# A decoder step's input projection started on two feature tiles, its RMS root multiplied in afterwards

## The chip, the cores and the metric

The kernel runs on one core of one Trainium2 chip. The metric is device time in microseconds (us) of one execution, the median of several. Everything is float32 in memory. A float32 product on TensorE is made of three passes: an operand is split into a high half (rounded to the `fp32r` format) and a low half (what the rounding left), and weights-high times data-high, weights-high times data-low and weights-low times data-high are added up in PSUM. The code calls these three matmuls a triple.

## The reference

One inference step of a one-layer decoder for 288 tokens: 256 of a prompt and 8 samples of 4 tokens. D is 2048. Cut to what the change touches:

```python
mod = silu(c) @ w_ada + b_ada             # 9 conditioning rows (prompt, 8 samples) -> 6 x 2048
sh_m, sc_m, gt_m, sh_f, sc_f, gt_f = mod  # shift, scale, gate for the mixer and for the FFN
h    = x * rsqrt(mean(x*x, -1) + 1e-6) * g_mix * (1 + sc_m) + sh_m
proj = h @ w_in                           # 288 x 2048 @ 2048 x 9216
...                                       # gated convolution, spatial gating, w_pa, w_pb, w_out
x    = x + gt_m * (merged @ w_out)
...                                       # second norm, SwiGLU FFN, residual, final norm
```

The mean of squares runs over the 2048 features of a token, so the root is one number for each token, and it needs all of `x`. Shift and scale are one number for each feature and conditioning row: one row for all prompt tokens, and one for each sample.

## The kernel before

Data lie transposed: 128 features on the partitions, 288 tokens along the free axis, so D is 16 *feature tiles*; `w_in` has 72 *output tiles* of 128 columns. A triple is one feature tile times one output tile (288 columns). Its product stands in one of four PSUM banks (`pm`) until a *sink* copies or adds it out; an output tile's partial sum is held in SBUF (`part[m]`, tiles named `s`).

The program is a list of steps. A `Blk` is a block of weights of 1 MB or less: one DMA on SP's queue into one of 7 buffers (`raw`), a *split* in pieces of four tiles (a cast `hi` on ScalarE, ACT, line 400, and a subtraction `lo` on VectorE, DVE, line 402), and its triples on TensorE, PE (lines 215 to 217). An `Ada` block is a piece of `w_ada`: its 4 to 16 float32 matmuls (line 336) add up in one PSUM bank, and the `tail` of the unit's last block copies it out (line 351), adds up its quarters by small matmuls (line 358) and writes `mod` (line 362). A `Do` is any other work, on PE between two triples; `later(f, gap)` holds it until `gap` triples are done. `warm(n)` puts n filler matmuls on data that nobody reads (line 461). A load is issued 7 steps ahead of its step, and a block is split one block ahead. PE's order is the program's. On ACT, DVE, POOL (GpSimd) and SP a scheduler sets it.

The input projection adds up over feature tiles as conditioning arrives, in passes named by their stream (first feature tile, feature tiles in a block, output tiles in a block):

```python
STREAMS = {
    "wA": (0, 1, 8),   # 48 output tiles, feature tile 0
    "wB": (1, 2, 8),   # the same 48, tiles 1 and 2
    "wX": (0, 3, 4),   # the other 24, tiles 0 to 2
    "wC": (3, 5, 3),   # all 72, tiles 3 to 7
    "wD": (8, 8, 2),   # all 72, tiles 8 to 15
```

Between blocks stand the conditioning units: aB in wA (tiles 1, 2), aC and aD in wB and wX (3 to 7), aE in wC (8 to 15).

**The head** is what comes before wA: `x` in four loads (2.36 MB), the two blocks of aA (shift and scale of tile 0 alone), then wA's first block. ACT squares `x` as it lands (line 469), DVE adds the squares up (line 474), PE sums them over the partitions by one-column float32 matmuls (line 481; a float32 matmul stands in the trace as two instructions, in the order below as one), DVE and POOL make the root (line 195), PE broadcasts it over the partitions (line 204), and ACT copies it to SBUF as `rb`, 128 x 288. Then `modulate` makes a tile of `h1`: x times `rb` on DVE (line 248), scale and shift on ACT for the prompt (line 259) and on DVE for the samples (lines 262, 263), the cast on ACT (line 265) and the low half on DVE (line 272). The sinks of wA are plain copies, half of them on ACT (line 521) and half on DVE (line 523); those of wB add (line 526).

Of the kernel before, what the change touches and what calls it, by code (L numbers as in the profile page):

```python
# [83 lines left out]
def _body(tc, nc, d, pc, pw, pslot, ptmp, pps):  # L84
# [166 lines left out]
    def modulate(ks, get, gm, sh0, out):  # L251
        hs, his = {}, {}

        def affine(k, t):
            h = tmp()
            hi = slot(F32R)
            if k == 0 and out is h1:
                A.activation(hi[:, :TP], t[:, :TP], AF.Identity, bias=mod[:, sh0 + k, 0:1], scale=gm[:, k, 0:1])
# [5 lines left out]
            if k == 0 and out is h1:  # L264
                A.copy(hi[:, TP:], h[:, TP:])
            else:
                A.copy(hi, h)
# [37 lines left out]
    class Ada(Step):  # L305
# [68 lines left out]
    class Blk(Step):  # L374
# [11 lines left out]
        cut = None  # L386
# [76 lines left out]
    def squares1():  # L463
        got = S["r1"] = {"ps": psmisc()}
        qs = []
        for a, b in zip(XCUT, XCUT[1:]):
            q = pw.tile([P, 2048], F32, tag="raw", name=nm("q"), bufs=RAW)
            q = q[:, : (b - a) * T].rearrange("p (k t) -> p k t", t=T)
            A.activation(q, x[:, a:b, :], AF.Square)
            qs.append(q)  # L470
        q = S["early"] = qs[0]
        S["late"] = qs[3]
        V.tensor_tensor(q, q, qs[1], ALU.add)
        V.tensor_tensor(q[:, 0:4], q[:, 0:4], qs[2], ALU.add)
        V.tensor_tensor(q[:, 0:2], q[:, 0:2], q[:, 2:4], ALU.add)

    def sums1(late):
        got = S["r1"]
        for q in [S["late"][:, i] for i in range(2)] if late else [S["early"][:, i] for i in (0, 1, 4)]:
            for tb, o in enumerate(TB):  # L480
# [4 lines left out]
                    start=not got.get("on"),  # L485
# [466 lines left out]
```

## Time and profile before

| what | value |
|---|---|
| device time, median of three runs | 1658.42 us (1657.89, 1658.42, 1658.43) |
| the profiled execution: device time | 1658.83 us |
| the profiled execution: span from its first to its last instruction | 1657.1 us |
| mean clock granted to PE, share of full speed | 0.991 |
| busy in the span: PE, DVE, ACT, POOL | 1633.0, 992.7, 745.1, 20.0 us |
| moved by DMA | 357.61 MB, mean 216 GB/s |
| chain that ended last, by engine | issue 52%, PE 46%, DMA 1%, DVE 1%, ACT 1% |

"Issue" in the chain is time in which the engine waited for nothing that the profile shows: here PE going from one matmul to the next. The page's row of 40 slices shows PE at 9 tenths or more from the second slice to the one before the last, with its clock at full; the first slice (41 us) and the last have 7, and the clock is lower there. Times in a timeline are counted from the span's start.

### The profile page before, as it was taken

Reading aid. Unit: us, or ns where it says so; the run is one execution under the profiler, and the core shown is the slowest. Engines: PE = TensorE matmul, PEld = TensorE weight load, DVE = VectorE, ACT = ScalarE, POOL = GpSimd, SP = SyncE. Lnnn points to the kernel's source line nnn. Section 1 sums busy time; section 2 is a strip of 40 time slices with the busy share of each in tenths; the row PEclk is TensorE's granted clock in tenths of the full one; section 3 lists DMA queues with packets and bytes.
Section 4 is the critical chain, followed back from the end, with each engine's and each line's share of the span. In section 5 each row is a group of like instructions: output and inputs, shape, how many; then the busy total and the mean of one; then the engine's idle time right before and its main releaser. Section 6 shows DMA issues by size and latency. Waiting matters only on the chain.

```text
span 1657.1 us, 31287 instructions
## 1 busy us (share of the span) xinstructions
PE 1633.0 (99%) x12559; PEld 1563.6 (94%) x12559; DVE 992.7 (60%) x2070; ACT 745.1 (45%) x1369; POOL 20.0 (1%) x62
## 2 busy tenths in 40 slices
PE   7999999999999999999999999999999999999997
PEld 6899999999899998999999999999999999999997
DVE  3775556877765566667944455555555555555565
ACT  4554335643444434446734444444444444344453
POOL 0000000000000000002000000000000000000000
PEclk7999999999999999999999999999999999999998
DMA  7876766666687667754487546543464434644341
GB/s 295 336 288 241 291 249 250 265 255 254 257 336 278 241 229 273 292 197 154 154 323 270 199 168 211 177 156 128 158 221 162 170 125 154 219 164 169 113 152 58
DMA packets 57122, 357.61 MB, mean 216 GB/s; under 512 B 6384, under 2 KB 9360, under 8 KB 24208
## 3 DMA queue, kind: packets, MB, share of 16 engines
q1 hardware_dynamic: 56688, 355.38, 58.5%
q8 instruction: 98, 1.61, 0.4%
q14 instruction: 48, 0.39, 0.1%
q10 hardware_dynamic: 288, 0.22, 0.0%
HBM read 352.49 MB, written 3.09 MB: 215 GB/s over the span
## 4 chain that ended last, share of the span: by engine, by line
issue 52%; PE 46%; DMA 1%; DVE 1%; ACT 1%; POOLq 0%; POOL 0%; ACTq 0%; DVEq 0%; SPq 0%
PE pm L215 14%; PE pm L216 13%; PE pm L217 13%; PE ada L336 4%; DMA raw<-in_wA 1%; DMA cp<-in_cpack 0%; DVE x L740 0%; PE px L358 0%; PE px L481 0%; PE px L204 0%; DVE lo L402 0%; ACT hi L400 0%; PE px L627 0%; PE px L629 0%; PE px L587 0%
## 5 line engine op out<-in xcount | busy, mean ns | idle before, releaser
L215 PE MATMUL pm<-s,hi 128*128 128x288 f32 (+1 forms) x3760 | 1112.2, 296 | 2.8 <-ACT s L521 1.5
L216 PE MATMUL pm<-s,hi 128*128 128x288 f32 (+1 forms) x3760 | 1107.7, 295 | 0.1
L217 PE MATMUL pm<-s,lo 128*128 128x288 f32 (+1 forms) x3760 | 1106.6, 294 | 0.0
L400 ACT CAST hi<-raw 128x512 fp32r<-128x512 f32 (+1 forms) x966 | 588.9, 610 | 814.6 <-PE pm L216 770.0
L402 DVE TENSOR_TENSOR lo<-raw,hi 128x512 fp32r<-128x512 f32 (+1 forms) x966 | 655.7, 680 | 478.2 <-ACT hi L400 459.0
L215 PEld LDWEIGHTS pm<-s,hi 128*128 128x128 f32 x3760 | 706.9, 188 | 21.1 <-issue 14.8
L217 PEld LDWEIGHTS pm<-s,lo 128*128 128x128 f32 x3760 | 706.7, 188 | 0.0
L216 PEld LDWEIGHTS pm<-s,hi 128*128 128x128 f32 x3760 | 706.1, 188 | 0.3 <-DVE s L272 0.3
L336 PE MATMUL ada<-raw,cs 128*32 128x512 f32 (+2 forms) x960 | 89.4, 517 | 0.0
L526 DVE TENSOR_TENSOR s<-pm,s 128x288 f32<-128x288 f32 x120 | 54.1, 454 | 40.5 <-PE pm L217 40.4
L336 PEld LDWEIGHTS ada<-raw,cs 128*32 128x32 f32 x960 | 28.7, 112 | 43.7 <-issue 38.5
L534 DVE TENSOR_TENSOR s<-pm,s 128x288 f32<-128x288 f32 x72 | 32.9, 456 | 15.0 <-PE pm L217 14.6
L241 ACT CAST s<-t 128x288 fp32r<-128x288 f32 (+1 forms) x76 | 32.6, 433 | 13.9 <-DVE t L566 6.7
L243 DVE TENSOR_TENSOR s<-t,s 128x288 fp32r<-128x288 f32 (+1 forms) x76 | 34.6, 459 | 6.8 <-ACT s L241 6.8
L288 DVE SCALAR_TENSOR_TENSOR x<-pm,mod,x 128x256 f32<-128x256 f32 x80 | 38.0, 475 | 0.0
L712 DVE SCALAR_TENSOR_TENSOR t<-t,pm 128x288 f32<-128x288 f32 x42 | 19.1, 454 | 16.6 <-PE pm L217 16.6
L287 DVE TENSOR_TENSOR t<-pm,mod 128x32 f32<-128x32 f32 x80 | 15.3, 192 | 21.3 <-PE pm L217 21.3
L154 ACT ACTIVATE t<-x 128x288 f32<-128x288 f32 x30 | 13.4, 446 | 20.8 <-DVE x L289 20.8
L159 DVE TENSOR_TENSOR acc<-acc,t 128x288 f32<-128x288 f32 x34 | 15.5, 456 | 8.2 <-ACT t L154 8.2
L521 ACT COPY s<-pm 128x288 f32<-128x288 f32 x45 | 17.0, 399 | 6.7 <-PE pm L217 6.7
L523 DVE COPY s<-pm 128x288 f32<-128x288 f32 x27 | 12.3, 456 | 11.5 <-PE pm L217 11.5
L259 ACT ACTIVATE t<-s,mod,gm 128x256 f32<-128x256 f32 x32 | 18.2, 596 | 2.1 <-DVE s L248 2.1
(110 smaller groups left out, 414.7 us busy)
## 6 DMA issues: line engine op xcount, KB each, us to landing
raw<-in_fi SPq DMA_DIRECT2D x84, 1024.0 KB, 4.9
raw<-in_a SPq DMA_DIRECT2D x64, 1024.0 KB, 9.8
raw<-in_f SPq DMA_DIRECT2D x64, 704.0 KB, 4.1
raw<-in_wD SPq DMA_DIRECT2D x36, 1024.0 KB, 4.9
raw<-in_wC SPq DMA_DIRECT2D x24, 960.0 KB, 4.8
raw<-in_aE SPq DMA_DIRECT2D x16, 1024.0 KB, 8.7
raw<-in_wo SPq DMA_DIRECT2D x16, 1024.0 KB, 5.1
raw<-in_aC SPq DMA_DIRECT2D x8, 1024.0 KB, 9.7
```

The costliest lines, as they stand in the source:

```text
L215: PE.matmul(out, wh, ah, start=first, stop=False)
L216: PE.matmul(out, wh, al, start=False, stop=False)
L217: lh = PE.matmul(out, wl, ah, start=False, stop=last)
L241: A.copy(hi, a)
L243: V.tensor_tensor(lo, a, hi.bitcast(F32), ALU.subtract)
L288: V.scalar_tensor_tensor(x[:, m, :TP], ps[:, :TP], mod[:, gt0 + m, 0:1], x[:, m, :TP], ALU.mult, ALU.add)
L336: PE.matmul(acc[32 * j : 32 * j + 32, :w], cs[:, kt, :], self.raw[:, o : o + w], start=(kt < ks), stop=(kt >= 16 - ks), tile_position=(0, ...
L400: A.copy(hi, self.raw[:, s * 128 : e * 128])
L402: V.tensor_tensor(lo, self.raw[:, s * 128 : e * 128], hi.bitcast(F32), ALU.subtract)
L526: V.tensor_tensor(part[m], ps[:, :T], part[m], ALU.add)
L534: V.tensor_tensor(a, ps[:, :T], a, ALU.add)
L712: V.scalar_tensor_tensor(t, t, 0.5, ps[:, :T], ALU.mult, ALU.mult)
```

## The change

1. *First unit of two tiles, ahead of x.* aA now makes shift and scale of tiles 0 and 1, in four blocks, and is loaded before `x`. aC has tiles 2 to 4, aD 5 to 7. `x` comes in five loads (tiles 0 and 1 first), and wA's first loads stand between them, cut in two or four. Fillers stand between the aA blocks.
2. *32 output tiles without the root.* wA takes feature tiles 0 and 1 for all 72 output tiles, in 9 blocks. In its first four blocks (32 output tiles) the data are `xe`: x times gain and scale, but not times the root (`mk_xe`). `xe` is 298 columns wide: behind the 288 tokens stand the 9 shifts (`mod`) and a zero. When the root is there, `rescale` on POOL multiplies each of these 32 results by `rb` (line 601) and adds the samples' shift column (line 602), in the program 8 tiles after each of wA's 5th to 8th block; `sinkC` adds the prompt's shift column.
3. *The root inside wA.* Squares and their adding are dealt out over the first three blocks (`pace`). PE's sums stand ten triples into wA[2], and the broadcast six triples after them, at wA[2]'s end. `norm1` then makes h1 of tiles 0 and 1, which wA[4] to wA[8] use.
4. *Passes over 2, 3 and 6 tiles.* Output tiles 48 to 71 go by wA, wB (tiles 2 to 4) and wX (5 to 7), tiles 0 to 47 by wA and wC (2 to 7). aC stands after wA's 6th and 8th block, aD after wB's 2nd and 4th. h1 of tiles 2 to 4 is made after wA's 8th block, of 5 to 7 after wB's 4th.
5. *Head in program order.* On ACT, DVE and SP the order is the program's until wA[3].
6. The first wD block runs over the first four feature tiles of both its output tiles, then over the other four (`run_outer`).

```diff
 ADA_UNITS = [
-    ("aA", (16, 16, 0, 0), 1, 8),
-    ("aB", (17, 17, 1, 1), 2, 4),
-    ("aC", (19, 21, 3, 5), 2, 2),
-    ("aD", (23, 23, 7, 7), 1, 8),
+    ("aA", (16, 16, 0, 0), 2, 4),
+    ("aC", (18, 18, 2, 2), 3, 2),
+    ("aD", (21, 21, 5, 5), 3, 2),
...
-EARLY = 48
-XCUT = (0, 5, 10, 14, 16)
+ROOTLESS = 32
+LATER = 48
+XCUT = (0, 2, 6, 10, 14, 16)
 STREAMS = {
-    "wA": (0, 1, 8),
-    "wB": (1, 2, 8),
-    "wX": (0, 3, 4),
-    "wC": (3, 5, 3),
+    "wA": (0, 2, 8),
+    "wB": (2, 3, 4),
+    "wX": (5, 3, 4),
+    "wC": (2, 6, 2),
...
     def squares1():
...
+        return {
+            (0, 5): square(q0, 0),
+            (1, 1): square(q1, 1),
+            (1, 3): add(q1[:, 0:2], q0),
+            (1, 4): square(q2, 2),
+            (1, 6): add(q1, q2),
+            (2, 1): square(q2, 3),
+            (2, 3): lambda: (square(q4, 4)(), add(q1, q2)()),
+        }
...
     def norm1():
         ps = rstd_bcast(S["r1"])
         S["rb1"] = ptmp.tile([P, T], F32, tag="rb", name=nm("rb"), bufs=1)
         A.copy(S["rb1"], ps)
-        xn[0] = normed(0, S["rb1"])
+        mk_h1(0, 2, False).run()
...
+    def mk_xe():
...
+        aA[3].tail(0, lambda: gm_of(0, 2), lambda: weights(1))
+        for f in (scaled, ends):
+            f(0)
+        rest(0)
+        scaled(1)
+        ends(1)
+        rest(1)
+        weights(1)
...
+    def rescale(m0, m1):
+        def f():
+            for m in range(m0, m1):
+                t = raws[m]
+                G.tensor_tensor(t[:, :T], t[:, :T], S["rb1"], ALU.mult)
+                G.tensor_tensor(sam(t[:, TP:T]), sam(t[:, TP:T]), bc4(t[:, T + 1 : T + NC]), ALU.add)
+
+        return Do(f, None)
+
+    def sinkC(m, ps):
+        if m not in raws:
+            return sinkB(m, ps)
+        t = raws.pop(m)
+        V.scalar_tensor_tensor(t[:, :TP], ps[:, :TP], t[:, T : T + 1], t[:, :TP], ALU.add, ALU.add)
+        V.tensor_tensor(t[:, TP:T], ps[:, TP:T], t[:, TP:T], ALU.add)
...
+    steps = [Do(lambda: warm(36)), aA[0], Do(lambda: warm(10)), aA[1], Do(lambda: warm(14)), aA[2], Do(lambda: warm(16)), aA[3]]
+    steps += [Do(mk_xe), Do(lambda: warm(10))]
+
+    def root():
+        later(sums1, 10)
+        later(norm1, 6)
+
+    plan = {2: [Do(root, None)], 6: aC[:4], 8: aC[4:] + [mk_h1(2, 5)]}
+    for i in range(4):
+        plan[5 + i] = [rescale(8 * i, 8 * i + 8)] + plan.get(5 + i, [])
+    steps += at(wA, plan)
+    steps += at(wB, {2: aD[:4], 4: aD[4:] + [mk_h1(5, 8)]})
+    steps += at(wX + wC, {3: aE[:4], 8: aE[4:8], 13: aE[8:12], 18: aE[12:] + [mk_h1(8, 12), mk_h1(12, 16)]})
...
+    first = wD(32, 40)
+    first[0].outer = True
...
+    head.enter_context(tc.manual_schedule(engines={A.engine, V.engine, SY.engine}))
+    for s in stream[:4]:
+        s.load()
+    stream[4].load(0, 512)
+    load_x(0)
+    stream[4].load(512)
+    S["paced"] = squares1()
+    stream[5].load()
+    load_x(1)
+    load_x(2)
+    stream[6].load()
+    load_x(3)
+    load_x(4)
     SY.dma_start(cp, d["cpack2"])
```

Three places in the order of instructions, of the kernel before and of the changed one. In these rows `ada` is aA's PSUM bank, `px` a PSUM bank for small work, `cp` holds packed constants, `q` the squares, `e` and `r` the root before and after the power, and `hi`, `lo` the halves of weights.

First place, PE, the root's sums and its broadcast. Before, between aA's matmuls (the rows left out between these are fillers):

```order
L481 MATMUL px_108<-ones,q_115 128x1 x6
L336 MATMUL ada_187<-raw_99,cs 32x128 x8
```

```order
L481 MATMUL px_108<-ones,q_109 128x1 x9
L336 MATMUL ada_187<-raw_99,cs 32x128 x8
L336 MATMUL ada_187<-raw_102,cs 32x128 x8
L204 MATMUL px_230<-cp_74,r_208 128x128 x2
L204 MATMUL px_230<-cp_74,r_208 128x32
L336 MATMUL ada_187<-raw_102,cs 32x128 x8
```

After, in wA[2], ten triples into it; six triples on, at its end, stands the broadcast:

```order
L218 MATMUL pm_528<-s_274,hi_490 128x298
L219 MATMUL pm_528<-s_272,lo_492 128x298
L514 MATMUL px_541<-ones,q_115 128x1 x12
L514 MATMUL px_541<-ones,q_116 128x1 x6
L217 MATMUL pm_564<-s_264,hi_490 128x298
L218 MATMUL pm_564<-s_266,hi_490 128x298
```

```order
L218 MATMUL pm_586<-s_274,hi_513 128x298
L219 MATMUL pm_586<-s_272,lo_515 128x298
L206 MATMUL px_595<-cp_74,r_560 128x128 x2
L206 MATMUL px_595<-cp_74,r_560 128x32
L217 MATMUL pm_624<-s_264,hi_537 128x298
L218 MATMUL pm_624<-s_266,hi_537 128x298
```

The sums and the broadcast have moved from between conditioning blocks to between triples, and triples are queued behind both; there are 18 one-column matmuls in place of 15.

Second place, DVE, where h1 of two tiles is made. Before, behind aB's tail (h1 of tiles 1 and 2):

```order
L504 SCALAR_TENSOR_TENSOR gm_89<-mod,cp_74 128x18
L248 TENSOR_TENSOR s_531<-x,rb_234 128x288
L248 TENSOR_TENSOR s_533<-x,rb_234 128x288
L262 TENSOR_TENSOR t_535<-s_531,gm_89 128x32
L402 TENSOR_TENSOR lo_585<-raw_396,hi_583 128x512
L263 TENSOR_TENSOR t_535<-t_535,mod 128x32
L262 TENSOR_TENSOR t_541<-s_533,gm_89 128x32
L263 TENSOR_TENSOR t_541<-t_541,mod 128x32
L272 TENSOR_TENSOR s_547<-t_535,s_536 128x288
L272 TENSOR_TENSOR s_549<-t_541,s_542 128x288
L523 COPY s_573<-pm_569 128x288
```

After, in wA[3] (h1 of tiles 0 and 1), ahead of the copies of wA[3]'s output tiles 24, 26 and 28:

```order
L250 TENSOR_TENSOR s_601<-x,rb_599 128x288
L250 TENSOR_TENSOR s_603<-x,rb_599 128x288
L262 TENSOR_TENSOR t_605<-s_601,gm_89 128x32
L263 TENSOR_TENSOR t_605<-t_605,mod 128x32
L262 TENSOR_TENSOR t_611<-s_603,gm_89 128x32
L263 TENSOR_TENSOR t_611<-t_611,mod 128x32
L404 TENSOR_TENSOR lo_679<-raw_188,hi_677 128x512
L269 TENSOR_TENSOR s_617<-t_605,s_606 128x288
L404 TENSOR_TENSOR lo_701<-raw_188,hi_699 128x512
L269 TENSOR_TENSOR s_619<-t_611,s_612 128x288
L595 COPY s_631<-pm_624 128x298
L595 COPY s_653<-pm_646 128x298
```

Both places have eight operations of h1; after the change they stand in front of the first copy of a block that has begun, with two splits among them, and the copy of output tile 24 frees the PSUM bank of tile 29, the sixth of the block.

Third place, POOL. Before, behind the root:

```order
L195 TENSOR_TENSOR r_208<-e_209,mhalf 128x3
L195 TENSOR_TENSOR r_4097<-e_4098,mhalf 128x3
L611 TENSOR_TENSOR s_6729<-s_6729,cp 128x256
L611 TENSOR_TENSOR s_6734<-s_6734,cp 128x256
L611 TENSOR_TENSOR s_6739<-s_6739,cp 128x256
```

After, behind the root:

```order
L197 TENSOR_TENSOR r_560<-e_561,mhalf 128x3
L601 TENSOR_TENSOR s_303<-s_303,rb_599 128x288
L601 TENSOR_TENSOR s_316<-s_316,rb_599 128x288
L602 TENSOR_TENSOR s_303<-s_303 128x32
L601 TENSOR_TENSOR s_325<-s_325,rb_599 128x288
L602 TENSOR_TENSOR s_316<-s_316 128x32
```

In front of the second norm's root there is now a row of 64 operations, 32 of each of the two lines, the first of which reads `rb` as soon as it is written.

## Rows read from the trace of the kernel before

**Rows 1.** The page's first section: busy us, share of the span, instructions.

```profile
PE 1633.0 (99%) x12559; PEld 1563.6 (94%) x12559; DVE 992.7 (60%) x2070; ACT 745.1 (45%) x1369; POOL 20.0 (1%) x62
```

**Rows 2.** Waits of PE: waiting engine and line, releaser, us, times, longest.

```profile
PE pm L215 <- ACT s L521: 1.5, 1, 1.5
...
PE pm L215 <- DVE s L526: 1.3, 1, 1.3
```

**Rows 3.** Windows: us, then PE, PEld, DVE, ACT, POOL busy; clock, DMA share, GB/s.

```profile
14.00:15.00 1.00, 0.00 (x0) 0.00 (x0) 0.00 (x0) 0.00 (x0) 0.00 (x0) 0.53 0.98 391
31.00:31.50 0.50, 0.50 (x4) 0.19 (x2) 0.13 (x1) 0.33 (x2) 0.00 (x0) 0.88 1.08 459
49.00:50.00 1.00, 0.00 (x0) 0.00 (x0) 0.77 (x3) 1.00 (x4) 0.00 (x0) 1.00 1.03 434
1000.00:1040.00 40.00, 40.00 (x304) 40.00 (x303) 22.66 (x50) 16.47 (x28) 0.00 (x0) 1.00 0.61 211
1645.00:1646.00 1.00, 0.00 (x0) 0.00 (x0) 0.16 (x1) 0.00 (x0) 0.76 (x1) 0.81 0.00 0
```

**Rows 4.** Timeline of the head: start, length, instructions [idle before <- releaser].

```profile
16.14 1.28 ACT L400 CAST hi<-raw 128x512 fp32r<-128x512 f32 x2 [5.25 <-DMA raw<-in_wA]
...
20.10 4.00 PE L481 MATMUL px<-ones,q 128*128 128x1 f32 x18 [6.60 <-DVE q L475]
...
27.61 1.08 PE L336 MATMUL ada<-raw,cs 128*32 128x128 f32 x16
...
31.88 0.19 PEld L216 LDWEIGHTS pm<-s,hi 128*128 128x128 f32 x1 [0.31 <-DVE s L272]
...
32.12 0.29 PE L217 MATMUL pm<-s,lo 128*128 128x288 f32 x1
```

**Rows 5.** The chain that ended last: start, length, engine, tile, line.

```profile
41.56 3.59 PE ada L336 x64
...
114.33 1.88 PE ada L336 x64
```

**Rows 6.** Timeline of ACT, in the head and from 40 us.

```profile
7.64 3.26 ACT L469 ACTIVATE q<-x 128x1440 f32<-128x1440 f32 x3 [0.77 <-DMA x<-in_x]
...
40.01 1.20 ACT L521 COPY s<-pm 128x288 f32<-128x288 f32 x3 [0.39 <-PE pm L217]
...
41.90 2.18 ACT L400 CAST hi<-raw 128x512 fp32r<-128x512 f32 x4
```

**Rows 7.** Timeline of DVE, in the head and from 42 us.

```profile
17.43 1.35 DVE L474 TENSOR_TENSOR q<-q,q 128x1152 f32<-128x1152 f32 x1
...
42.55 2.50 DVE L402 TENSOR_TENSOR lo<-raw,hi 128x512 fp32r<-128x512 f32 x4 [0.89 <-ACT hi L400]
...
47.25 0.82 DVE L248 TENSOR_TENSOR s<-x,rb 128x288 f32<-128x288 f32 x2
...
48.69 0.18 DVE L263 TENSOR_TENSOR t<-t,mod 128x32 f32<-128x32 f32 x1
```

**Rows 8.** Timeline of PE, round sums, a broadcast and wider triples.

```profile
329.42 0.72 PE L179 MATMUL px<-ones,acc 128*128 128x1 f32 x6
330.00 0.38 PE L215 MATMUL pm<-s,hi 128*128 128x288 f32 x1
...
791.50 0.30 PE L215 MATMUL pm<-s,hi 128*128 128x298 f32 x1
...
792.75 0.94 PE L204 MATMUL px<-cp,r 128*128 128x128 f32 x6
```

**Rows 9.** Timeline of POOL and DVE; last, line 402's durations, ns, min/median/max.

```profile
505.48 0.74 POOL L611 TENSOR_TENSOR s<-s,cp 128x256 f32<-128x256 f32 x1 [20.27 <-DMA s<-in_wsg]
...
735.49 0.24 POOL L679 TENSOR_TENSOR t<-x,gm 128x32 f32<-128x32 f32 x1 [4.46 <-DVE x L289]
...
505.70 1.07 DVE L402 TENSOR_TENSOR lo<-raw,hi 128x512 fp32r<-128x512 f32 x1
...
L402 DVE TENSOR_TENSOR lo<-raw,hi x99: 681/691/694, 300.7 to 479.8; 128x512 fp32r<-128x512 f32 x99
```

More of the change, by code (lines that the diff above doesn't have):

```diff
@@ L1 @@
+import contextlib
 import numpy as np
@@ L263, in affine @@
             V.tensor_tensor(sam(h[:, TP:]), sam(h[:, TP:]), bc4(mod[:, sh0 + k, 1:]), ALU.add)
[L264 to L267, printed above, removed]
+            A.copy(hi, h)
             hs[k], his[k] = h, hi
@@ L346, in run, with tail @@
                 self.tail()
-        def tail(self, gap=3):
+        def tail(self, gap=3, scaled=None, copied=None):
             w, ks, acc = self.nq * 128, self.ks, Ada.cur[self.name]
@@ L413, in run, with run_outer @@
                 self.sink(self.idx * self.nm + j, ps)
+                if self.pace:
+                    self.pace(j)
                 drain()
+        def run_outer(self):
+            pss = [psmain() for _ in range(self.nm)]
+            h = self.nk // 2
+            for k0 in (0, h):
+                for j, ps in enumerate(pss):
+                    for k in range(k0, k0 + h):
+                        triple(ps[:, :T], self.parts[j * self.nk + k], self.rhs(self.k0 + k), k == 0, k == self.nk - 1)
+            for j, ps in enumerate(pss):
+                self.sink(self.idx * self.nm + j, ps)
+            drain()
     class KBlk(Blk):
@@ L463, in squares1, with part_of, square, add @@
     def squares1():
-        got = S["r1"] = {"ps": psmisc()}
[L465 to L479, printed above, removed]
+        qa, qb = (pw.tile([P, 2048], F32, tag="raw", name=nm("q"), bufs=RAW) for _ in range(2))
+        for q in (qa, qb):
+            G.memset(q[:, 7 * T : 7 * T + 1], 0.0)
+        def part_of(q, o, n):
+            return q[:, o * T : (o + n) * T].rearrange("p (k t) -> p k t", t=T)
+        q1, q0, q2, q4 = part_of(qa, 0, 4), part_of(qa, 4, 2), part_of(qb, 0, 4), part_of(qb, 4, 2)
+        def square(q, i):
+            return lambda: A.activation(q, x[:, XCUT[i] : XCUT[i + 1], :], AF.Square)
+        def add(o, q):
+            return lambda: V.tensor_tensor(o, o, q, ALU.add)
+        S["sq"] = [q1[:, i] for i in range(4)] + [q4[:, i] for i in range(2)]
+        return {
[7 more added lines that the diff above has]
+        }
+    def sums1():
+        got = S["r1"] = {"ps": psmisc()}
+        qs = S.pop("sq")
+        for i, q in enumerate(qs):
             for tb, o in enumerate(TB):
@@ L514, in mk_h1, with gm_of @@
+    def gm_of(k0, k1):
+        V.scalar_tensor_tensor(
+            gm1[:, k0:k1, :],
+            mod[:, 16 + k0 : 16 + k1, :],
+            1.0,
+            gmix[:, k0:k1].unsqueeze(2).to_broadcast([P, k1 - k0, NC]),
+            ALU.add,
+            ALU.mult,
+        )
+    def mk_h1(k0, k1, gm=True):
+        def f():
+            if gm:
+                gm_of(k0, k1)
+            modulate(range(k0, k1), lambda k: normed(k, S["rb1"]), gm1, 0, h1)
         return Do(f)
-    part = {}
+    part, raws = {}, {}
@@ L833, in _body @@
             and nxt <= cur + 1
-            and not (blks[nxt].defer and blks[nxt] is not s)
+            and (blks[nxt] is s or not (blks[nxt].pace or getattr(s, "pace", None)))
         ):
-            blks[nxt].split()
+            if not blks[nxt].pace:
+                blks[nxt].split()
             nxt += 1
```

128 lines of the change are left out of this document (73 added, 55 removed).

## The prediction

> **What bounds the kernel now.** I read the busy shares first: TensorE (PE) is busy in 1633 of 1657.1 us [rows 1]. A busy PE isn't yet PE at work, since fillers and waits inside a matmul count, so the next view is what PE waits for. After the first triple there are two waits of weight, 1.5 and 1.3 us, where products stand in all four PSUM banks and ScalarE (ACT) or VectorE (DVE) hasn't copied one out [rows 2]. From then on PE sets the pace: 304 matmuls of 288 columns in 40 us [rows 3], 0.132 each, so a triple takes 0.395 us and 16 of them 6.3. What PE can be spared is the head. The third real matmul stands at 32.12 us [rows 4]; at 0.132 each the stream starts in effect at **31.86 us**.
>
> The head is a chain of loads. The first piece of wA lands at 16.1 us, behind all of x and aA: 4.9 MB [rows 4]. Then the root's sums and aA's tail follow on one path; the last aA matmuls begin at 27.61 and take 1.08 us [rows 4], at about half clock (0.53 in the us from 14, and back to 0.88 only in the half us from 31) [rows 3].
>
> **The change, part by part.**
>
> *The head.* Four aA loads (4.2 MB) go first, then a piece of wA and two tiles of x. x[0:2] is complete at byte 4.97 MB, about where the first wA piece stood, so I put both at 16.2 us. aA's end lies 0.53 MB earlier; at 391 GB/s [rows 3] that is 1.35 us: 14.8. Its last block is 8 matmuls of 256 columns, a quarter of the 3.59 us that 32 take (64 rows) [rows 5]: 15.7. Before, 3.2 us passed from the end of aA (28.69) to the second matmul, which waits for the low half (31.88) [rows 4]. Now one ACT pass falls away (taken as a cast, 0.55, a quarter of 2.18 [rows 6]) and a weight split stands ahead on DVE (0.63, a quarter of 2.50 [rows 7]): 19.0. The second feature tile needs one more pass on ACT and one on DVE, 0.9 to 1.0: 19.9, by when four matmuls (0.5) are done. The stream starts in effect at **19.4**, and 12.5 us are gained. Fillers between the aA blocks fill PE's waits, so I take full clock.
>
> *Work moved on PE.* Twice as much of aA lies ahead of the stream, so 1.9 us of ada matmuls less come after it [rows 5]. The 18 sums, in slack before, now stand between triples: 36 rows at six in 0.58 us (329.42 to 330.00) make 3.5 [rows 8]. The broadcast of the root adds 1.0 [rows 8]. The first 64 triples have 298 columns: 192 matmuls at 0.139 (nine from 791.50 to 792.75) [rows 8] in place of 0.132 add 1.3. The two waits of 2.8 belong to blocks that are gone. So -12.5 - 1.9 + 3.5 + 1.0 + 1.3 - 2.8 = **-11.4 us**, if nothing new waits. The other passes (2, 3 and 6 tiles) hold the same 576 triples, and the other order in the first wD block changes no count: nothing, since PE covers them. sinkC adds an operation of some 0.2 us to 32 sinks on DVE, under 4.7 us of PE for each block of 12 triples: nothing. Of DMA I charge nothing either: the aC loads wait for the squares' buffers until the sums are done near 41 us, 3.1 MB take 8 us at the rate above, and PE wants them near 68.
>
> *What waits anew.* Four places.
>
> (a) The sums stand in wA[2] behind ten triples (4.2 us into the block), and everything behind them on PE waits too. They wait for the last adding of squares. Its chain starts with PE's fourth triple (1.7), since ACT's copy of that tile stands ahead: copy 0.40, square of 1152 columns 1.2, cast 0.55 [rows 6], then on DVE a split 0.63 and the adding 1.35 [rows 7]: 5.8. Wait: **1.6**.
>
> (b) From there PE has 1.6 us of nothing and 3.5 of one-column matmuls. At the kernel's end, where PE had the same sums and waits behind its last triple, the clock falls in the stretch from 1645 (0.81), and in the head it fell at 14 after sums, few fillers and waits; in the wait of 1.5 it stayed at 1.00 [rows 3]. So I take it to fall one us ahead of the sums' end: ten rows at 0.22 in place of 0.10 (18 rows took 4.0 at half clock [rows 4]) and some 2.5 us of triples at half speed, as long as the head's fillers and first matmuls needed from 28.7 to 31: 1.3 + 1.2 = **2.5**; 0 if it holds, 3.8 if it falls early in the sums.
>
> (c) wA[3]. The broadcast root releases two feature tiles of h1 on DVE and ACT, and on both queues they stand ahead of the copies that free PSUM banks (second place shown under the change). Without POOL: ACT's copy of the second tile stands behind a cast that needs eight triples done (3.3), then 0.55 + 0.4 + 0.4 = 4.7, where PE has done four tiles by 3.3: wait 1.4. But the same root releases 32 rescalings on POOL. They read two SBUF operands, as most of DVE's operations here do. In the trace such a POOL operation of 256 columns takes 0.74, and a split on DVE that starts 0.22 into it takes 1.07 where the median is 0.69 [rows 9]: DVE got the rest only when POOL had ended. A rescaling of 288 columns is then 0.83 and its small partner 0.24 [rows 9]. Ten such DVE operations (3.6 us of their own: four of 0.41, four of 0.18, two splits of 0.63 [rows 7]) with five long POOL ones between, some 0.74 of each in the way (3.7), put the copy of the first tile at 0.5 + 3.6 + 3.7 = 7.8, and PE wants that bank for its sixth tile at 4.2. Wait: **3.6**, bounds 1.4 and 4.5.
>
> The Trainium skill has this as a rule, against the change: in SBUF — State Buffer, Who interferes with whom, a VectorE instruction with two SBUF inputs and a GpSimd instruction that reads SBUF exclude each other for a whole instruction. The trace agrees (1.07 against 0.69). By the same section an instruction with one SBUF input, as the PSUM copies, stays free, and the sum is as above.
>
> (d) wA[8] holds mk_h1(2, 5) behind aC's second half. The same sum for its sixth tile (the gating cast at 3.8, then 2.7 of ACT work, against 4.6 of PE): 1.9 without POOL, 4.9 with it all along. POOL starts near 45; 32 tiles of 1.07 make 34 us, and DVE's splits hold it up for about 11, so it ends near 90, and wA[8] begins near 86. Nearer the low end: **2.5**. For mk_h1(5, 8), under two wB blocks whose sinks stand between, 0.3.
>
> Between, in wA[4] to wA[7], DVE has a split and a copy (0.63 + 0.40) and up to 0.4 of POOL in each 1.58 of PE: covered, at 90%.
>
> **Sum.** 1.6 + 2.5 + 3.6 + 2.5 + 0.3 = 10.5, and -11.4 + 10.5 = **-0.9 us**. The profiled execution took 1658.83, its span 1657.1 and 1.7 around it; the median of the three runs is 1658.42. The span would come to 1656.2, the profiled run to 1657.9, the median to **1657.5**.
>
> **The rivals.**
>
> *Little of it waits.* If POOL doesn't hold DVE and the clock stays up, the waits are 1.6 + 1.4 + 1.9 + 0.3 = 5.2: -6.2, **1652.2**. If one of the two is there, 7.7 to 8.0: **1654.9**. For it: PE held 1.00 through the waits before. Against it: the stretched splits.
>
> *POOL isn't done in time (slower).* Its place is wA[8]. It decides from 1.3 us a tile, waits included (32 in the 41 us from 45 to 86): then POOL goes on through wA[8], (d) is 4.9, (c) its upper 4.5, and both waits are long enough for the clock to fall in them too, 1.2 each; with (b) at 3.8 the waits are 17.5: +6.1, **1664.5**. For it: DVE is at 90% there, and each split stops POOL for 0.6. Against it: under the eight aC blocks DVE has little to do.
>
> *The head doesn't start early.* If x[0:2] or wA land 3 us later than the bytes say (on SP they stand behind loads whose semaphores they reuse), the stream starts at 22.4: +2.1, **1660.5**. The loads waited for are the first aA blocks, landed long before, so I give it little.
>
> **How the numbers follow.** A measurement here can tell about 0.2% (3.3 us) from no change. Forecast 0.42, with 1654.4 to 1660.4 as its own range and some of its weight past either bound of no change; little waits 0.36 (faster); POOL late 0.14 (slower); head late 0.08 (the same or slower). Faster 0.38, the same 0.44, slower 0.18. To leave out 2 in 10 the range goes from below the low rival, 1650.5, to near the high one, 1663.5.
>
> **What would show it.** In the profile after: the first triple at 18 to 19 us; no gap between fillers and aA blocks; a PE wait for the adding of squares near 36 to 38, then a granted clock below 1.00 near 40; POOL busy some 34 us from 45 on; splits of up to 1.1 us on DVE in that time; PE waits of 3 us in all in wA[3] for a DVE copy, and one near 90 for an ACT copy. A first triple past 21, a clock of 1.00 throughout, or splits that stay at 0.69 would make the prediction wrong, each by its own term.

## The result, and the profile after

The changed kernel takes 1665.03 us in the median of 18 runs (1660.25 to 1666.88), the kernel before 1658.38 (1657.63 to 1658.76). The ratio is **1.0036, 95% interval 1.0029 to 1.0043: slower by 6.6 us**, where 1657.5 was forecast with no change as the likeliest outcome. The time lies above the whole range. The profiled execution took 1665.84, its span is 1664.0, 6.9 more than before.

The page's first section answers to [rows 1]: PE is busy for 10.4 us more, with the same triples.

```profile
PE 1643.4 (99%) x12466; PEld 1568.3 (94%) x12466; DVE 998.5 (60%) x2087; ACT 740.1 (44%) x1355; POOL 59.5 (4%) x128
```

PE's waits, as [rows 2] before (columns: us in all, times, longest). The first line is two waits, of 2.3 in wA[3] and 2.1 in wA[8], the second stands ahead of the root's sums, the third again in wA[3]:

```profile
PE pm L217 <- ACT s L593: 4.4, 2, 2.3
PE px L514 <- DVE q L496: 1.6, 1, 1.6
...
PE pm L217 <- DVE s L595: 1.3, 1, 1.3
```

The timeline of PE (start, length):

```profile
16.52 1.07 PE L333 MATMUL ada<-raw,cs 128*32 128x256 f32 x16
...
20.25 0.37 PE L217 MATMUL pm<-s,hi 128*128 128x298 f32 x1 [0.31 <-ACT s L538]
...
22.09 0.30 PE L217 MATMUL pm<-s,hi 128*128 128x298 f32 x1
...
40.37 7.54 PE L514 MATMUL px<-ones,q 128*128 128x1 f32 x36 [1.59 <-DVE q L496]
47.77 0.59 PE L217 MATMUL pm<-s,hi 128*128 128x298 f32 x1
48.17 0.45 PE L218 MATMUL pm<-s,hi 128*128 128x298 f32 x1
...
58.52 0.41 PE L217 MATMUL pm<-s,hi 128*128 128x298 f32 x1 [2.30 <-ACT s L593]
...
60.97 0.43 PE L217 MATMUL pm<-s,hi 128*128 128x298 f32 x1 [1.35 <-DVE s L595]
...
103.20 0.40 PE L217 MATMUL pm<-s,hi 128*128 128x288 f32 x1 [2.08 <-ACT s L593]
```

And windows round the sums and round wA[3] (columns as in [rows 3]; the third number from the end is the granted clock):

```profile
39.00:40.00 1.00, 0.00 (x0) 0.00 (x0) 1.00 (x2) 0.72 (x2) 0.00 (x0) 1.00 0.00 0
40.00:41.00 1.00, 0.63 (x5) 0.63 (x5) 1.00 (x3) 0.00 (x0) 0.00 (x0) 0.86 0.79 254
41.00:42.00 1.00, 1.00 (x6) 1.00 (x6) 0.29 (x1) 0.00 (x0) 0.00 (x0) 0.50 0.90 369
...
50.00:51.00 1.00, 1.00 (x6) 1.00 (x5) 0.00 (x0) 1.00 (x3) 0.00 (x0) 0.52 0.88 369
51.00:52.00 1.00, 1.00 (x10) 1.00 (x9) 0.86 (x2) 0.27 (x2) 0.00 (x0) 1.00 0.43 172
...
61.00:62.00 1.00, 1.00 (x5) 1.00 (x6) 0.66 (x2) 0.00 (x0) 1.00 (x3) 0.60 0.00 0
...
65.00:66.00 1.00, 1.00 (x9) 1.00 (x8) 0.21 (x1) 0.86 (x2) 1.00 (x3) 1.00 0.00 0
102.00:103.00 1.00, 0.00 (x0) 0.00 (x0) 0.78 (x4) 0.66 (x3) 0.00 (x0) 1.00 1.04 436
104.00:105.00 1.00, 1.00 (x9) 1.00 (x9) 0.25 (x2) 0.83 (x2) 0.00 (x0) 1.00 1.03 430
```

What the reader is to see: the clock is full while PE waits at 39, and falls 0.4 us into the sums. It stays at half through the rest of the 36 rows (7.4 us from 40.37 to 47.77, where 3.5 were reckoned for full clock), and through the first triples behind them, until 51. It falls once more behind the two waits of wA[3], from 61 to 65. Behind the wait of wA[8] it stays full in this execution; in others it does not (below). A mean clock of 0.992 hides this, because the clock of before (0.991) has its low stretch in the old head.

### The profile page after: what moved, and what is told of

Same layout as the page of the kernel before. It is cut to its first block, busy times and chain, and to the rows that moved or that the text cites. A ratio compares the mean times of both kernels' runs of the same rounds, so it can differ in the third digit from the quotient of the medians.

```text
span 1664.0 us, 31217 instructions
## 1 busy us (share of the span) xinstructions
PE 1643.4 (99%) x12466; PEld 1568.3 (94%) x12466; DVE 998.5 (60%) x2087; ACT 740.1 (44%) x1355; POOL 59.5 (4%) x128
## 3 DMA queue, kind: packets, MB, share of 16 engines
q8 instruction: 97, 1.59, 0.4%
## 4 chain that ended last, share of the span: by engine, by line
issue 51%; PE 46%; DVE 2%; ACT 0%; POOL 0%; POOLq 0%; DVEq 0%; ACTq 0%
PE pm L217 13%; PE pm L218 13%; PE pm L219 13%; PE ada L333 4%; PE pm L480 1%; DVE lo L404 1%; PE px L514 0%; DVE x L828 0%; PE px L358 0%; ACT hi L402 0%; DVE s L269 0%; DVE s L250 0%; PE px L715 0%; PE px L717 0%; PE px L675 0%
## 5 line engine op out<-in xcount | busy, mean ns | idle before, releaser
L217 PEld LDWEIGHTS pm<-s,hi 128*128 128x128 f32 x3760 | 708.5, 188 | 25.8 <-issue 16.1
L333 PEld LDWEIGHTS ada<-raw,cs 128*32 128x32 f32 x832 | 24.2, 109 | 46.1 <-issue 44.5
L197 POOL TENSOR_TENSOR r<-e,mhalf 128x3 f32<-128x3 f32 x4 | 3.4, 855 | 1149.5 <-DVE e L196 1102.5
L622 DVE TENSOR_TENSOR s<-pm,s 128x288 f32<-128x288 f32 x72 | 32.9, 457 | 15.7 <-PE pm L219 15.6
L614 DVE TENSOR_TENSOR s<-pm,s 128x288 f32<-128x288 f32 x64 | 29.1, 455 | 19.2 <-PE pm L219 17.9
L601 POOL TENSOR_TENSOR s<-s,rb 128x288 f32<-128x288 f32 x32 | 29.3, 916 | 4.2 <-ACT rb L527 4.2
L595 DVE COPY s<-pm 128x288 f32<-128x288 f32 (+1 forms) x36 | 16.2, 456 | 12.1 <-PE pm L219 12.1
L593 ACT COPY s<-pm 128x288 f32<-128x288 f32 (+1 forms) x36 | 14.2, 399 | 16.8 <-PE pm L219 16.8
```

What stands on the lines that cost most here:

```text
L217: PE.matmul(out, wh, ah, start=first, stop=False)
L333: PE.matmul(acc[32 * j : 32 * j + 32, :w], cs[:, kt, :], self.raw[:, o : o + w], start=(kt < ks), stop=(kt >= 16 - ks), tile_position=(0, ...
L601: G.tensor_tensor(t[:, :T], t[:, :T], S["rb1"], ALU.mult)
L614: V.tensor_tensor(part[m], ps[:, :T], part[m], ALU.add)
L622: V.tensor_tensor(a, ps[:, :T], a, ALU.add)
```

## The experiments

Each was timed beside the kernel before on the same chip. Ratios are to the kernel before, with 95% intervals; the changed kernel stands at 1665.03 and 1.0036 [1.0029, 1.0043]. A profile is of one execution, in e1, e5 and e7 of the fastest or nearly the fastest of the run, so times are compared by medians, waits and clock by profiles.

| run | us | ratio |
|---|---|---|
| e1_fill | 1662.14 | 1.0027 [1.0018, 1.0036] |
| e2_no_rescale | 1660.70 | 1.0014 [1.0006, 1.0023] |
| e3_fill_no_rescale | 1660.67 | 1.0013 [1.0004, 1.0021] |
| e4_head | 1664.73 | 1.0032 [1.0021, 1.0044] |
| e5_spread | 1663.17 | 1.0027 [1.0017, 1.0037] |
| e6_rescale_late | 1661.18 | 1.0018 [1.0009, 1.0028] |
| e7_h1_apart | 1666.15 | 1.0046 [1.0033, 1.0058] |
| e9_one_column_run (on the kernel before) | 1665.52 | 1.0043 [1.0031, 1.0056] |
| e10_few_sums | 1656.83 | 0.9993 [0.9984, 1.0002] |
| e11_few_sums_late | 1655.61 | 0.9982 [0.9973, 0.9991] |
| e12_few_14 | 1658.08 | 0.9997 [0.9988, 1.0005] |
| e13_early_aC | 1655.50 | 0.9983 [0.9974, 0.9992] |
| e14_few_no_wait | 1653.53 | 0.9970 [0.9958, 0.9982] |
| e15_run_no_wait | 1659.22 | 0.9999 [0.9990, 1.0008] |

The theory at the start: the clock falls for PE's wait ahead of the sums, and POOL's multiplications make the waits in wA[3]. The rivals: the sums themselves bring the clock down; the order of h1 ahead of the copies makes the waits alone; the head is held back by its fillers.

**Fillers in the wait.**

```diff
     def sums1():
+        extra = psmisc()
+        for _ in range(12):
+            PE.matmul(extra[:, :T], wb[:, :P], wb, start=True, stop=True)
```

> Twelve fillers of 0.13 us each stand ahead of the root's sums in wA[2], in PE's wait for the last adding of squares (1.6 us in the changed kernel). If that wait is what lets PE's clock fall, it holds now: the sums' 36 rows take 3.5 us instead of 7.4, and the 13 half-speed matmul gaps behind them (1.5 us) go: 5.4 us less, 1659.6 us. If the one-column matmuls themselves let it fall, it falls again within or after them: a gain of 0 to 1.0, 1664.0 to 1665.0. The waits in wA[3] (2.3 and 1.3) stay in both.

1662.14, so neither. The wait is gone from the trace, and the clock falls all the same, this time in the middle of the sums. Timeline and windows of PE:

```profile
37.85 1.65 PE L514 MATMUL px<-wb 128*128 128x288 bf16 x12
39.59 5.28 PE L517 MATMUL px<-ones,q 128*128 128x1 f32 x36
44.73 0.59 PE L217 MATMUL pm<-s,hi 128*128 128x298 f32 x1
```

```profile
41.00:42.00 1.00, 1.00 (x11) 1.00 (x11) 0.00 (x0) 0.00 (x0) 0.00 (x0) 1.00 0.66 277
42.00:43.00 1.00, 1.00 (x8) 1.00 (x9) 0.00 (x0) 0.00 (x0) 0.00 (x0) 0.72 0.08 31
43.00:44.00 1.00, 1.00 (x6) 1.00 (x6) 0.00 (x0) 0.00 (x0) 0.00 (x0) 0.50 0.47 80
```

PE counts as busy for all of that time. The first theory falls in its simple form: filling the wait doesn't keep the clock up. How much the fillers brought is open: the intervals overlap, and with POOL's work left out they brought nothing (next).

**Without POOL's multiplications**, alone and with the fillers. The edit takes `rescale` out of the plan, so the kernel leaves out the root for 32 output tiles.

```diff
-        plan[5 + i] = [rescale(8 * i, 8 * i + 8)] + plan.get(5 + i, [])
+        plan[5 + i] = plan.get(5 + i, [])
```

> Leaves out the multiplication of the first 32 output tiles by the root and the samples' shift (64 POOL operations), nothing else. If POOL's operations stretch those of DVE and so hold back the copies in wA[3], PE's waits there fall from 3.65 to 1.4 us or less, the clock doesn't fall behind them (1.6), and the wait in wA[8] goes from 2.1 to 1.9 or less: some 4 us less, 1661.0 us. If the order of h1 ahead of the copies on ACT and DVE makes the waits alone, they stay: 1664.5 to 1665.5 us. The sums keep their 7.4 us in both.

> Both edits: fillers ahead of the sums, and the multiplication of the first 32 output tiles by the root left out (with the samples' shift). If both causes are real and independent, the gains add up: 5.4 + 4.1, 1655.5 us, faster than the kernel before (1658.4). If the second fall of the clock hangs on the first, or the waits are the order's, between 1657 and 1661 us.

1660.70 and 1660.67: the 4 us of POOL's theory are there, the sum of both is not. First DVE's operations of h1, in the changed kernel beside POOL's (timeline of both engines) and then line 263's durations (ns, min/median/max):

```profile
55.44 0.80 POOL L601 TENSOR_TENSOR s<-s,rb 128x288 f32<-128x288 f32 x1
...
55.56 0.73 DVE L263 TENSOR_TENSOR t<-t,mod 128x32 f32<-128x32 f32 x1
...
L263 DVE TENSOR_TENSOR t<-t,mod x2: 718/725/732, 55.6 to 56.5; 128x32 f32<-128x32 f32 x2
```

The same line without POOL's multiplications, and PE's waits there:

```profile
L263 DVE TENSOR_TENSOR t<-t,mod x2: 191/192/192, 51.4 to 51.8; 128x32 f32<-128x32 f32 x2
...
PE pm L217 <- ACT s L593: 3.3, 2, 2.1
```

An operation that takes 0.19 starts 0.12 into one of POOL's and ends with it, after 0.73. Without POOL the wait in wA[3] is 1.2 (3.3 less the 2.1 of wA[8]) in place of 3.65, and the clock stays at 1.00 behind it. The wait in wA[8] is as long as before: POOL had no part in that. That the clock falls behind the waits of wA[3] can't be put down to POOL alone: with POOL's work in place it stays at 1.00 behind 2.9 us of waits there in e1's profile and 3.1 in e7's. And in e2 and e3 it falls behind the wait of wA[8] instead, for 3.4 us from 96.2 and 96.6.

**The head's fillers.**

```diff
-... aA[0], Do(lambda: warm(10)), aA[1], Do(lambda: warm(14)), aA[2], Do(lambda: warm(16)), aA[3]]
+... aA[0], Do(lambda: warm(9)), aA[1], Do(lambda: warm(9)), aA[2], Do(lambda: warm(9)), aA[3]]
```

> Between the aA blocks 9, 9 and 9 fillers in place of 10, 14 and 16. If the fillers hold the last aA block back (by the bytes moved it has landed near 14 to 15 us, and it starts at 16.52 right behind a filler), it starts 13 fillers of 0.13 earlier, and so does the stream: 1.7 us less, 1663.3 us. If the loads come no earlier than the fillers let them be used, PE waits in their place: the start stays (1665.0), and up to 2 us are lost where the clock falls in those waits (1667).

1664.73, no change. PE now waits for the loads (timeline of PE):

```profile
13.29 0.64 PE L333 MATMUL ada<-raw,cs 128*32 128x256 f32 x8 [0.43 <-DMA raw<-in_aA]
...
15.88 0.64 PE L333 MATMUL ada<-raw,cs 128*32 128x256 f32 x8 [0.17 <-DMA raw<-in_aA]
```

PE waits for the last half megabyte of aA until 15.88; the prediction's bytes had it there at 14.8.

**The sums in six pieces, a triple between each two.** `sums1` issues three matmuls and puts the next three behind one triple; `norm1` stands three triples behind the last.

> The root's sums in six pieces of three matmuls, a triple between each two, from the tenth triple of wA[2] on; the broadcast stands three triples behind the last piece, two triples into wA[3]. If a long run of one-column matmuls is what lets PE's clock fall, it holds now: the 36 rows take 3.5 us in all (7.4 in the profile of the changed kernel, 5.1 to 5.6 in others) and no triple is slow behind them (1.5): 4 to 5 us less, 1660.5 us. If it is the wait ahead of them, or anything else in that place, the clock falls as before: 1664 to 1666.

1663.17, and the interval overlaps that of the changed kernel: about 2 us at best, and not certain. The six pieces (timeline of PE) take 0.83 and 0.73 at first, and 1.27 from 43.35 on, where the clock has gone to half in spite of the triples between:

```profile
39.98 0.83 PE L515 MATMUL px<-ones,q 128*128 128x1 f32 x6 [1.59 <-DVE q L496]
41.18 0.73 PE L515 MATMUL px<-ones,q 128*128 128x1 f32 x6
42.26 0.72 PE L515 MATMUL px<-ones,q 128*128 128x1 f32 x6
43.35 1.27 PE L515 MATMUL px<-ones,q 128*128 128x1 f32 x6
```

The wait of 1.59 stands ahead of the sums here too, so this run shows only that a triple between each two pieces doesn't keep the clock up.

**POOL's multiplications later.**

```diff
+    def gate():
+        z = tmp()[:, 0:1]
+        V.tensor_scalar(z, h1[7][1][:, 0:1].bitcast(F32), 0.0, None, ALU.mult)
+        A.activation(S["rb1"], S["rb1"], AF.Identity, bias=z)
...
-    steps += at(wB, {2: aD[:4], 4: aD[4:] + [mk_h1(5, 8)]})
+    steps += at(wB, {2: aD[:4], 4: aD[4:] + [mk_h1(5, 8)], 5: [Do(gate, None), rescale(0, 32)]})
```

> The 32 multiplications by the root run on POOL only from the end of wB on, once h1 of tiles 5 to 7 is there (the broadcast root is rewritten in place with a zero that hangs on it, two small operations more). If only POOL's coincidence with h1 in wA[3] costs, this gives what leaving the multiplications out gave: 1660.7 us. If their work costs wherever it stands, since DVE is stretched there too, 1662 to 1665.

As in e2, `rescale` is taken out of wA's plan too. 1661.18, as when the multiplications are left out: POOL runs from 137 us on and no wait of PE comes of it. It is their place beside h1 that costs, not their work.

**h1 of the tiles apart.** `norm1` makes h1 of tile 0 and puts tile 1 three triples behind it; behind wA's 8th block, tiles 2, 3 and 4 are three triples apart.

> h1 of tile 1 three triples behind that of tile 0, and h1 of tiles 2, 3 and 4 three triples apart, so that copies that free PSUM banks come between. If the order of h1 ahead of the copies makes the waits, the one in wA[8] (2.1 us) shrinks to under 0.5 and those in wA[3] (3.65) to about 2: 3 to 4 us less, 1661.5. If DVE's and ACT's work as such is too much for these blocks, the waits only move, some to the end of the block where the next needs the last h1 tile: 1664 to 1666.

1666.15, no gain. PE's waits for ACT's copies are now four, and 4.8 us in place of 4.4; the second row is DVE's:

```profile
PE pm L217 <- ACT s L594: 4.8, 4, 2.1
...
PE pm L217 <- DVE s L596: 1.0, 1, 1.0
```

In wA[3] they are 3.1 in place of 3.65, in wA[8] 2.7 in place of 2.1: the waits have moved, as the other side of that expectation said.

**A run of one-column matmuls alone, in the kernel before.**

```diff
+    def one_column():
+        ps = psmisc()
+        for i in range(6):
+            for tb, o in enumerate(TB):
+                PE.matmul(
+                    ps[:, tb : tb + 1], x[:, i, o : o + 128], ones[:, 0:1],
+                    start=i + tb == 0, stop=False, skip_group_check=True,
+                )
+
-    steps += at(wC, {3: aE[:4], ...
+    steps += at(wC, {1: [Do(one_column, None)], 3: aE[:4], ...
```

> The kernel before, with 18 one-column float32 matmuls (36 rows) on x put in one run behind the first wC block, far from the head; all that they read has long been there, and nobody reads the result. If such a run by itself lets the clock fall, it costs 5 to 9 us (36 rows at full clock are 3.5, at half 7.4, and 1.5 for slow triples behind): 1663.5 to 1667.5. If it takes a wait ahead of them, they cost 3.5: 1662.0.

1665.52, 7.0 us more. Timeline of PE, then windows:

```profile
140.99 0.29 PE L217 MATMUL pm<-s,lo 128*128 128x288 f32 x1
141.12 4.98 PE L773 MATMUL px<-ones,x 128*128 128x1 f32 x36
145.96 0.59 PE L215 MATMUL pm<-s,hi 128*128 128x288 f32 x1
```

```profile
143.00:144.00 1.00, 1.00 (x11) 1.00 (x10) 0.00 (x0) 0.00 (x0) 0.00 (x0) 1.00 0.69 123
144.00:146.00 2.00, 2.00 (x12) 2.00 (x11) 0.00 (x0) 0.00 (x0) 0.00 (x0) 0.52 0.91 376
...
148.00:150.00 2.00, 2.00 (x10) 2.00 (x10) 0.06 (x1) 0.62 (x1) 0.00 (x0) 0.50 0.00 0
150.00:152.00 2.00, 2.00 (x14) 2.00 (x14) 1.00 (x2) 0.49 (x1) 0.00 (x0) 0.77 0.00 0
```

No wait stands ahead of the run, PE counts as busy all through, and the clock falls within it, 2.9 us after it began, and stays at half for 6.8 us. All five executions are 6.3 us or more above the kernel before, where the rows alone are 3.5. So the sums themselves are enough; whether a wait alone is enough too, this run can't say. (The Trainium skill, in TensorE: Matmul & The Clock Gate, HAM oscillation — how this bites in real kernels, speaks of idle gaps of PE as what brings the clock down; by this run a PE that counts as busy can lose it too, and the measurement decides.)

**Fewer sums.** DVE adds the squares up to one tile; the sums are 6 rows.

```diff
-        S["sq"] = [q1[:, i] for i in range(4)] + [q4[:, i] for i in range(2)]
+        S["sq"] = [q1[:, 0]]
...
+            (2, 4): add(q1[:, 0:2], q1[:, 2:4]),
+            (2, 5): add(q1[:, 0:2], q4),
+            (2, 6): add(q1[:, 0], q1[:, 1]),
...
-        later(sums1, 10)
-        later(norm1, 6)
+        later(sums1, 18)
+        later(norm1, 3)
```

> DVE adds the six tiles of squares up to one (three more operations, dealt out over wA[2]), so that PE's run of one-column matmuls is 6 rows in place of 36; it stands 18 triples behind wA[2]'s start in place of 10, the broadcast three triples behind it. POOL's multiplications stay where they were. If the long run is what lets the clock fall, the run takes 0.6 us (7.4), the slow triples behind it go (1.5), and so does the wait ahead of it (1.7): 8 to 10 us less than the changed kernel's 1665.0, 1655 to 1657, faster than the kernel before. If something else in that stretch makes the clock fall, it still does: 1659 to 1661.

1656.83, 8.2 less than the changed kernel and in the range of the long run's theory, but not for that theory's reasons, so the match is luck. The longer adding keeps PE waiting for 2.0 us even at 18 triples, and the clock still falls, at 44.1, as that wait ends. The sums and PE's wait in wA[3] (timeline of PE):

```profile
44.16 1.44 PE L517 MATMUL px<-ones,q 128*128 128x1 f32 x6 [1.99 <-DVE q L496]
...
54.06 0.40 PE L217 MATMUL pm<-s,hi 128*128 128x298 f32 x1 [0.83 <-ACT s L596]
```

The two profiles are 7.2 us apart. The 30 rows less give 2.9 of that, and 6.8 us at half clock in place of 10.2 give 1.7. As much comes from elsewhere: the broadcast stands five triples later, so the copy of wA[3]'s first tile is done before h1 begins, the waits there are 0.83 in place of 3.65, and no fall comes behind them (1.7). Against this stand 0.4 more ahead of the sums, 0.5 more in wA[8] and a fall behind that wait (1.7). That is 6.5 of the 7.2.

Three runs on that footing, all with POOL's multiplications late:

> The same fewer sums, and POOL's multiplications from the end of wB on. If the two causes are independent, the gains add up: another 3.9 us less, 1651 to 1653. If POOL's cost was one of the clock that had fallen already, the second edit brings under 1 us more: 1655 to 1656.

1655.61, only 1.2 less than the run before and in the second range: the gains don't add up. The profiles say why: with h1 made five triples later, POOL's work costs PE 1.0 us of waits in all (0.83 and 2.60 in wA[3] and wA[8] with it, 0.31 and 2.09 without), where it had cost 2.4 in wA[3] of the changed kernel.

> As the one before, but the sums 14 triples behind wA[2]'s start and the broadcast five behind them. The last adding ends at about 7.5 us (18 triples), so PE waits 1.6 us ahead of the sums, and h1 of tiles 0 and 1 comes 0.8 us earlier. If only the wait counts: 1.6 us more than at 18 triples. If h1 is late for wA[4] at 18, the same or less. The clock stays in both, if a wait of this length doesn't bring it down; if it does, 3 us more.

The broadcast's gap is the only other edit (14 and 5 triples in place of 18 and 3). 1658.08, 2.5 more than at 18: more than the wait's 1.6, less than with 3 more for the clock. The wait ahead of the sums is 3.7 in place of 2.0, and in the profile the clock falls 0.5 before it ends, where in e11 it falls 1.2 after the sums' start.

> As the run with fewer and later sums and late multiplications, with both halves of aC one block of wA earlier, so that h1 of tiles 2 to 4 is made under wA[7] and has wA[8] as well to be ready. If the wait of 2.1 us behind it comes from copies that stand behind h1, it only moves into wA[7]: no change. If it is DMA that aC then waits for, 1 to 3 us more.

The edit is `5: aC[:4], 7: aC[4:] + [mk_h1(2, 5)]` in place of 6 and 8. 1655.50, no change, and a wait of 2.1 for ACT's copy stands one block earlier: it moved, as the first half of that expectation had it.

**What is enough for the fall.** In these runs a wait and a few rows stood together. Two runs with 40 output tiles without the root move the sums 24 triples behind wA[2]'s start, with nothing to wait for: one with 6 rows (its edit below, against e11), one with all 36 rows (without the edit to the adding, against e6).

```diff
-ROOTLESS = 32
+ROOTLESS = 40
...
-        later(sums1, 18)
-        later(norm1, 3)
+        later(sums1, 24)
+        later(norm1, 4)
...
-... 5: [Do(gate, None), rescale(0, 32)]})
+... 5: [Do(gate, None), rescale(0, 40)]})
```

> As the run with fewer sums and late multiplications (1655.6), with 40 output tiles multiplied without the root in place of 32, the sums' 6 rows 24 triples behind wA[2]'s start, when the last adding has long ended, and the broadcast four behind them. If in that run the clock fell for PE's wait of 2.15 us ahead of the sums, wait and fall both go: 2.15 for the wait and some 1.6 for triples at half clock, less 0.4 for 16 wider triples: 1652.2. If 6 rows and the broadcast are enough by themselves, it falls again: 1653.8 or more.

> 40 output tiles without the root and late multiplications, with all 36 rows of sums in one run 24 triples behind wA[2]'s start, with no wait ahead of them; to be read against the run with late multiplications alone (1661.2). If the run is enough in this place too, the clock falls as there, and only the wait of 1.7 us goes: 1659.9. If wait and run are both needed here, the sums take 3.5 us and no triple is slow: 1656.

1653.53, between the two values expected, and 1659.22. Windows round the sums in e11 (6 rows at 43.68, behind a wait of 2.0):

```profile
43.00:44.00 1.00, 0.32 (x3) 0.32 (x3) 1.00 (x4) 0.00 (x0) 0.00 (x0) 1.00 0.67 92
...
45.00:46.00 1.00, 1.00 (x6) 1.00 (x5) 0.31 (x1) 0.43 (x1) 1.00 (x1) 0.50 1.29 424
```

In e14 (6 rows at 44.72, no wait ahead of them):

```profile
45.00:46.00 1.00, 1.00 (x9) 1.00 (x10) 0.64 (x2) 0.71 (x2) 0.28 (x1) 1.00 0.85 342
...
48.00:49.00 1.00, 1.00 (x8) 1.00 (x9) 1.00 (x4) 0.43 (x2) 0.00 (x0) 1.00 0.86 317
```

Further on in e14, the wait of wA[8] (timeline of PE) and a window behind it:

```profile
88.68 0.40 PE L217 MATMUL pm<-s,hi 128*128 128x288 f32 x1 [2.09 <-ACT s L596]
```

```profile
90.00:91.00 1.00, 1.00 (x6) 1.00 (x5) 0.52 (x1) 0.75 (x2) 0.00 (x0) 0.50 0.84 350
```

In e15 (36 rows at 44.75, no wait):

```profile
47.00:48.00 1.00, 1.00 (x11) 1.00 (x11) 0.00 (x0) 0.00 (x0) 0.00 (x0) 1.00 0.63 258
48.00:49.00 1.00, 1.00 (x7) 1.00 (x7) 0.00 (x0) 0.00 (x0) 0.00 (x0) 0.54 0.52 104
```

So in this place, as in e9, the long run is enough by itself, in the execution that was profiled (1659.36). Five of the eleven executions of e15 take 1655.8 to 1657.1, near the 1656 expected for a clock that holds, so the fall need not come each time. Six rows without a wait were not enough in e14's profile.

A wait is enough without any sums. In e10 the clock falls as the wait of 2.0 ends, in e12 within the wait of 3.7. Thirteen profiles have a wait of 2.1 to 2.6 in wA[8] (in e13 in wA[7]), with triples on both sides. In eight of them (e2, e3, e6, e10, e11, e13, e14, e15) the clock falls 0 to 1.4 us after that wait and stays at half for 3.4 us, which costs 1.7; in five (the changed kernel, e1, e4, e5, e12) it stays full. No run here shows what decides between them.

**e14 beats both kernels**: 4.9 us, or 0.3%, under the kernel before, with the wait of wA[8] and the fall behind it still in its profile.

## Why the prediction was wrong, step by step

The sums below are of the profiled execution, read from the starts of successive matmuls.

- **The bound.** Right: PE sets the pace, and every term is one of PE's.
- **The head, −12.5.** It was −10.6: the seventh matmul starts at 22.09, so at 0.139 each the stream starts in effect at 21.26, not 19.4. The steps from aA's end to the stream were right (17.59 to 21.26 is 3.67, reckoned 3.7). What failed is aA's landing: with the fillers out of the way it is at 15.88 in e4, 1.1 later than the rate of 391 GB/s gave, and in the profiled execution the fillers put the last block at 16.52 (15.4 to 16.1 in most other runs' profiles). Why it lands later is not shown. In e2's profile, with the same head, the last block starts at 15.38 and the stream in effect at 20.2.
- **Work moved.** Right: −1.8 for the conditioning matmuls (four groups of 2.72), 0.9 for the broadcast.
- **(a) the wait for the squares, 1.6.** Right to the decimal: 1.59.
- **(b) the clock, 2.5. This is the step that failed.** It put the fall one microsecond ahead of the sums' end, and the rows show it at their start: 7.4 − 3.5 = 3.9 for the sums and 1.5 for the triples behind, 5.4 in all. My bound of 3.8 for an early fall was too low by my own numbers (36 rows at 0.12 more are 4.3, and 1.2 behind them 5.5). The reason was wrong too: it took wait and sums together to bring the clock down near the sums' end, and so most of the sums as done at full clock. A run of 36 one-column rows brings it down by itself, without any wait (e9, e15), and a wait by itself can do so too (e10, e12). And the clock stays down longer than the 2.5 us behind the sums that were reckoned. In the five profiles with this wait and these sums the fall begins 0.4 to 3.0 us into the sums and lasts 10.2 us (the changed kernel, e4, e6) or 6.8 (e2, e7). At half clock that is 5.1 or 3.4 us, both more than 2.5. The rows that I had read for this, at the kernel's end and in the old head, have sums and waits together, and could not tell.
- **(c) wA[3], 3.6.** Right in size and in cause: 2.30 + 1.35, of which POOL's multiplications make 2.4 (e2). What is missing is the fall behind it, 1.6 us between 61 and 64.5. I had priced that in the rival alone, at 1.2. It is in e4's profile too, and not in those of e1 and e7.
- **(d) wA[8], 2.5.** 2.08, near its low end, and not POOL's: e2 has the same wait. A fall behind it, again priced in the rival alone, stays away in this profile and comes in eight others, at 1.7. h1 of tiles 5 to 7 cost nothing under wB, where 0.3 was put; instead, in the first wD block, the low half of a late h1 tile cost 0.8 by starts of matmuls.
- **The sum.** 1.9 too little in the head, 2.9 in (b), 1.6 for the second fall and 0.5 for the last h1 are 6.9, less 0.4 in (d). That is 6.5 of the 7.8 between −0.9 and +6.9; the rest was not traced to its places.
- **The rivals.** None came true as it stood. The time is that of the slower one (1664.5), and two of its three parts are there, (b) early and a fall behind a wait; but its mechanism isn't: POOL ended near 93 without holding up wA[8].
- **The chances.** The forecast gave (b) one value, and the range its bounds; what it is changes from one execution to the next. A spread of 6.6 us between executions of the changed kernel, where the kernel before has 1.1, goes with the mean clock (0.994 to 0.995 in the four runs under 1661.5, 0.990 to 0.993 in the others). In the profiles the fall begins 0.4 us into the sums (the changed kernel) or 2.3 (e2, with the same sums and the same wait).

## What to carry to other kernels

When work that lay in a slack head is moved between the matmuls of the main stream, ask of every PE instruction not only how long it takes but what it does to the clock of those behind it: here 36 one-column rows cost 3.5 us of their own and up to 5.4 more in clock. Add up on another engine first, so that PE's run is short, and place it where nothing has to be waited for: a wait of 2 us alone was followed by a fall in most profiles, and a fall cost 1.7 or more. And put POOL's two-operand work where DVE has no chain that PE waits for; the same work some 80 us later cost nothing that these runs can tell. The three together, with 8 more output tiles without the root, turned a loss of 6.6 us into a gain of 4.9.

## What was not expected of the hardware

- A run of 36 one-column float32 matmul rows lets PE's granted clock fall to half with PE counted as busy throughout, 143.00 to 144.00 at 1.00 and 144.00 to 146.00 at 0.52 in e9, and it costs 7.0 us in a kernel that has no other change, 3.5 of them for the rows. With single triples between pieces of 6 rows, behind a wait of 1.6, it fell as well (e5).
- A wait of PE of 2.1 us (2.6 in e10) with triples at full clock ahead of it was followed by a fall to 0.50 for 3.4 us in e14 and seven other profiles, and by none in five.
- A DVE operation on 32 columns waits out a POOL operation on 288, both reading two operands in SBUF (0.19 becomes 0.73, ending with it). It is as with the split's 1.07 in [rows 9], here with a POOL operation four times as long as DVE's own time.
